# Up projection of a gated MLP by seven block products in place of eight, with the gated features kept in DRAM

## The chip, the cores and the metric

One core of a Trainium2 chip. The metric is the device time of one execution in microseconds, as the median of several runs. Engines are named as in the profile: PE is TensorE's matmul and PEld its weight load, DVE is VectorE, ACT is ScalarE, POOL is GpSimd, SP is SyncE, whose queue issues every transfer of this kernel.

## The reference

The kernel computes two layers of a diffusion backbone over 1024 latent tokens and 256 context tokens of width 1024, all in fp32. A layer is a mixing sub-layer (one input projection, four head groups, one output projection) and a channel sub-layer, both inside scaled RMS norms. Only the channel sub-layer of the latents changes:

```
def conv_ffn(h, w_up, w_conv, w_down):          # h (1024, 1024)
    u = dwconv3(h @ w_up, w_conv)               # w_up (1024, 2 * 2816), width-3 convolution over tokens
    a, b = jnp.split(u, 2, -1)
    return (jax.nn.silu(a) * b) @ w_down        # w_down (2816, 1024)
hx = rmsnorm(x, g_pre_ffn[l]) * (1 + s2_x) + sh2_x
x = x + g2_x * rmsnorm(conv_ffn(hx, ...), g_post_ffn[l])
```

The first layer does the same for the context tokens; the second layer doesn't need them.

## The kernel before

Every fp32 product is made of three TensorE passes. Both operands are split into a rounded part and a residual (`weight`, L109, for weights: ScalarE casts RAW to WH at L116, VectorE subtracts to WL at L117; `to_hk`, L247, for activations), and `project` (L286) adds hi x hi, hi x lo and lo x hi in PSUM at L291 to L293. A moving operand has 512 token columns, a stationary one 128 x 128.

**Entering the MLP.** `out_tile` (L1049) finishes the output projection of one tile of 128 tokens: norm, gate, residual sum, store to `xmid`, and the norm in front of the MLP. `to_h2` (L1085) turns four such tiles for one slice k of 128 features: four transposes on PE (L251), scale and shift on ACT (L252), cast and residual on DVE (L253, L254). The first token half is written after tiles 5 and 6 and behind the loop over tiles, the second half at its end (L1110 to L1116).

**The MLP of the latents.** The features come in 22 pairs f of 128 gate and 128 value features. `up` (L1150) computes a pair: for each of the two, `fmajor` (L295) runs two token halves of 8 slices x 3 matmuls into the two PSUM tiles G, ACT copies them out (L1158), `conv3` (L321) makes the convolution with one pass on ACT (L324) and two on DVE (L325, L326). SiLU (L1164), product (L1165) and the split of the gated features (L1167, L1168) follow; they stay in SBUF. `down` (L1233) takes groups of two pairs and, for each of the eight token tiles, adds 2 x 2 x 3 matmuls (L1174 to L1176) into a PSUM tile M2, which DVE adds to an SBUF accumulator `acc` (L1254). Up and down alternate by groups. After the last group come Square, the gate product (split between POOL and DVE, L1262) and the sum with `xmid` (L1213); the very last tile of the kernel goes by halves (`end_tile`, L1216).

**Beside it.** In the first layer `mod_pool` (L158) computes the next layer's modulation in steps between the tiles of `down`: 24 blocks of 1 MB, four matmuls each (L182). `ctx_h2` (L1135) and the loop at L1304 make the context's MLP behind that of the latents, and there the next layer's norms and transposes begin (`Prenorm`).

**Order.** The source emits instructions in the order told; the build then arranges each engine's queue from that order, the dependencies and its own estimate of when each input is ready, so that a queue's order need not be the source's. At run time a queue is worked off strictly in order. Buffers are pools of named tiles with fixed counts: RAW 3, WH and WL 4 each, G 2, HC 2.

Of the kernel before, what the change touches and what calls it, by code (L numbers as in the profile page):

```python
# [9 lines left out]
ALU = mybir.AluOpType  # L10
# [15 lines left out]
LG = 4  # L26


def build(tc, d, out, dbg=None):
# [19 lines left out]
    xmid = [[dram.t([P, D], f"xmid{l}_{t}") for t in range(NT + 2)] for l in range(DEPTH)]  # L49
    xres = [[dram.t([P, D], f"xres{l}_{t}") for t in range(NT + 2)] for l in range(DEPTH - 1)]  # L50
# [107 lines left out]
    def mod_pool(m, ts, w_tile, r_tile, ahead):  # L158

        l = m.l
        work = [(t, k) for t in ts for k in range(KT)]
        ws = {}

        def load(i):
            if i < len(work):
                t, k = work[i]
                w = ws[i] = w_tile()  # L170
                sp.dma_start(out=w, in_=d["w_mod"][l, P * k : P * k + P, 2048 * t : 2048 * t + 2048])

        for i in range(ahead):
            load(i)
        pr = None
        for i, (t, k) in enumerate(work):
            load(i + ahead)
            w = ws.pop(i)
            if k == 0:
                pr = X()  # L180
            for j in range(4):
                pe.matmul(pr[32 * j : 32 * j + 32, :], sc32[:, k, :], w[:, 512 * j : 512 * j + 512], start=(k == 0), stop=(k == KT - 1))  # L182
            yield
            if k == KT - 1:
                mr = r_tile()
                act.copy(mr, pr)
                yield
                yield
                mod_out(m, t, mr)
            else:  # L190
                yield
                yield
            yield

    def mod_out(m, t, mr):
        tp = X()
# [63 lines left out]

    def h_tiles():
        hh = [hp_.t([P, N], "H", 16, F32R) for _ in range(KT)]
        hl = [hp_.t([P, N], "H", 16, F32R) for _ in range(KT)]
        return hh, hl

    def hc_tiles():
        return hp_.t([P, KT, NC], "HC", 2, F32R), hp_.t([P, KT, NC], "HC", 2, F32R)

# [591 lines left out]
    for l in range(DEPTH):  # L860
# [136 lines left out]
        korder = [2, 3, 4, 5, 6, 7, 0, 1]  # L997
        wop = Pool(f"wo{l}", bufs=1, side="right")
        wo = {}

        def load_wo(kk, early):
# [4 lines left out]
            else:  # L1006
                hi, lo = hp_.t([P, N], "H", 16, F32R), hp_.t([P, N], "H", 16, F32R)
# [72 lines left out]
        hh2, hl2 = [], []  # L1080
        for k in range(KT):
            hh2.append(hp_.t([P, N], "H", 16, F32R))
            hl2.append(hp_.t([P, N], "H", 16, F32R))

        def to_h2(n0, k, ps):  # L1085
            ns = slice(P * n0, P * n0 + 512)
            to_hk(k, xn[n0 : n0 + 4], hh2[k][:, ns], hl2[k][:, ns], m.a2, m.mc[:, 3], 0, tmp2(), ps)
# [8 lines left out]
        for i, t in enumerate(order):  # L1096
# [13 lines left out]
            if t in (5, 6):  # L1110
                for k in (2 * t - 10, 2 * t - 9):
                    to_h2(0, k, G())
        for k in range(4, KT):
            to_h2(0, k, M2()[:, 0:512])
        for k in range(KT):
            to_h2(4, k, M2()[:, 0:512])  # L1116
# [4 lines left out]
        psum_phase(f"d{l}", X=1, M2=2, M1=1)  # L1121
        if l + 1 < DEPTH:
            m2 = mods[l + 1] = mod_cols(l + 1)
            mod_small(m2)

            it2 = mod_pool(m2, (0, 1, 2), lambda: hp_.t([P, 2048], "HC", 2), lambda: hp_.t([P, 512], "HC", 2), 1)
# [8 lines left out]
        def ctx_h2(fpool, tpool):  # L1135
# [4 lines left out]
            for i, t in enumerate((8, 9)):  # L1140
# [6 lines left out]
                     lambda: fpool.t([P, 128], "t1", 1), mx)  # L1147
# [30 lines left out]
        halves = [slice(512 * i, 512 * i + 512) for i in range(2)]  # L1178


        tpool = Pool(f"ft{l}", bufs=1, side="right")
        if with_ctx:
            cpool = Pool(f"fc{l}", bufs=1, side="right")
        fpool = Pool(f"ff{l}", bufs=1, side="left")
        tk, tkc = Tok(hh2, hl2), None
        acc = [fpool.t([P, D], "acc", NT) for t in range(NT)]
        gs, fin, ahead = {}, [], {}


        spare = not with_ctx  # L1190
        if spare:
            lp = Pool(f"lp{l}", bufs=1, side="right")

        def g_tiles(f):
            if spare and f > FF - LG:
                hc = hp_.t([P, 2, N], "HC", 2, F32R) if f < FF - 1 else lp.t([P, 2, N], "g", 1, F32R)
                return hc[:, 0], hc[:, 1]
            return fpool.t([P, N], "gh", 3, F32R), fpool.t([P, N], "gl", 3, F32R)

        def up_l(f):  # L1200
            gs[f] = up(f, tk, LAT, N, tpool, g_tiles)

        def load_x(t):
            if t < NT:
                ahead[t] = tpool.t([P, D], "T4", 3)
                sp.dma_start(out=ahead[t], in_=xmid[l][t])

        def close(t, r):

            if t not in ahead:  # L1210
                load_x(t)
            x = ahead.pop(t)
            dve.scalar_tensor_tensor(x, acc[t], r[:, 0:1], x, ALU.mult, ALU.add)  # L1213
            sp.dma_start(out=xres[l][t] if l + 1 < DEPTH else out[P * t : P * t + P], in_=x)

        def end_tile(t, pt, sq, gt2):  # L1216

            x = ahead[t]
            ss = sm.t([P, 4], "ss2")
            for i, h in enumerate(halves):  # L1220
                dve.tensor_add(acc[t][:, h], pt[:, h], acc[t][:, h])
                act.activation(sq[:, h], acc[t][:, h], AF.Square, accum_out=ss[:, i : i + 1])
            while fin:
                close(*fin.pop(0))
            for e, h in zip((pool, dve), halves):
                e.tensor_mul(acc[t][:, h], acc[t][:, h], gt2[:, h])
            dve.tensor_add(ss[:, 2:3], ss[:, 0:1], ss[:, 1:2])
            r = rstd_of(ss[:, 2:3])
            for h in halves:
                dve.scalar_tensor_tensor(x[:, h], acc[t][:, h], r[:, 0:1], x[:, h], ALU.mult, ALU.add)  # L1230
                sp.dma_start(out=out[P * t : P * t + P, h], in_=x[:, h])

        def down(fs, first, last):  # L1233
            if last:
                gt2 = fpool.t([P, D], "gh", 3)
                gate_tile(m, 1, 0, gt2)
                sq = fpool.t([P, D], "gl", 3)
                if spare:
                    load_x(0)
            wd = {f: weight(d["w_down"][l, P * f : P * f + P, :]) for f in fs}  # L1240
            for t in range(NT):
                if last and spare:
                    load_x(t + 1)
                pt = M2()
                for ns in halves:
                    for i, f in enumerate(fs):
                        down_into(pt[:, ns], ns, gs[f], wd[f], slice(P * t, P * t + P), i == 0, i == len(fs) - 1)
                if last and t == NT - 1 and l + 1 == DEPTH:
                    end_tile(t, pt, sq, gt2)
                    return  # L1250
                if first:
                    act.copy(acc[t], pt)
                else:
                    dve.tensor_add(acc[t], pt, acc[t])  # L1254
                for _ in range(2 - (t % 4 > 0)):
                    next(it2, None)
                if last:
                    ss = sm.t([P, 1], "ss")
                    act.activation(sq, acc[t], AF.Square, accum_out=ss)
                    cut = 384 if spare else 768  # L1260
                    for e, c in ((pool, slice(0, cut)), (dve, slice(cut, D))):
                        e.tensor_mul(acc[t][:, c], acc[t][:, c], gt2[:, c])  # L1262
                    fin.append((t, rstd_of(ss, tag="f")))
                    if len(fin) > DELAY:
                        close(*fin.pop(0))
            if last:
                while fin:
                    close(*fin.pop(0))

        DELAY = 2 if l + 1 < DEPTH else 1  # L1270
        n = FF - LG if spare else FF
        groups = [list(range(f, f + FG)) for f in range(0, n, FG)] + ([list(range(n, FF))] if spare else [])
        for f in groups[0]:
            up_l(f)

        for gi, fs in enumerate(groups):
            nx = groups[gi + 1] if gi + 1 < len(groups) else []
            if nx:
                up_l(nx[0])
            early = spare and gi == len(groups) - 2  # L1280
            if early:
                for f in nx[1:]:
                    up_l(f)
            if with_ctx and gi == len(groups) - 2:
                tkc = ctx_h2(fpool, tpool)
            down(fs, gi == 0, not nx)
            if not early:
                for f in nx[1:]:
                    up_l(f)
        fpool.close()  # L1290
        if spare:
            lp.close()
# [3 lines left out]
        if with_ctx:  # L1296
            nf = Prenorm(l + 1, m2, Pool(f"nm{l + 1}", bufs=1, side="left"), xres[l], mx)
# [130 lines left out]
```

## Time and profile before

| | |
|---|---|
| median of three runs | 2830.73 us (2830.61 to 2831.06) |
| the profiled execution, its own time | 2831.68 us |
| its span | 2829.8 us |
| PE busy | 2761.1 us (98%) |
| DVE, ACT, POOL busy | 1483.0, 1019.6, 130.8 us |
| share of the chain that ended last | PE 78%, DVE 4%, ACT 2%, DMA 2% |
| moved by transfers | 271.27 MB, mean 96 GB/s |

The span reaches from the first to the last instruction of the profiled execution; its own time is measured around it. A group of instructions is told as line, engine, operation, output <- input, shape, count, then busy time and mean duration of one, then the engine's idle time ahead of them. The durations of matmuls overlap, since TensorE works on several at a time. A stretch of the table of stretches is told with busy time and instructions of each engine, the granted clock of TensorE (1.00 is full), the transfer engines' share and GB/s.

### The profile page before, as it was taken

The numbers are of one execution on the slowest core, as the hardware profiler recorded it, in microseconds if no ns is written. First come the engines' busy times: TensorE is split into PE (matmuls) and PEld (weight loads), VectorE is DVE, ScalarE is ACT, GpSimd is POOL, SyncE is SP. The second block draws the span as 40 slices with busy tenths as digits, with TensorE's granted clock in tenths as the row PEclk, the third lists the DMA queues.
The fourth block names the chain that finished last, engine by engine and source line by source line (L and its number), as shares of the span: only waits on it lengthen the run. The fifth ranks groups of instructions, "written<-read, shape, count | busy, mean of one in ns | idle before, by whom it ended". The sixth has DMA issues, their size and how long they took to land.

```text
span 2829.8 us, 36199 instructions
## 1 busy us (share of the span) xinstructions
PE 2761.1 (98%) x14624; PEld 2262.9 (80%) x14624; DVE 1483.0 (52%) x2459; ACT 1019.6 (36%) x1697; POOL 130.8 (5%) x158
## 2 busy tenths in 40 slices
PE   7999999999999999999899999999999999999998
PEld 4877888887778777777789898788878888888886
DVE  5445456445344444444788754466453444544455
ACT  5222435334322222222467522345344323232331
POOL 0003000000000000000120001100000000000002
PEclk9999999999999999999999999999999999999999
DMA  6631222532222222322386520312521111111113
GB/s 250 212 117 44 64 55 53 181 131 76 90 78 83 100 88 72 95 90 59 120 271 198 178 78 20 89 45 62 195 81 52 45 53 45 52 45 52 45 51 121
DMA packets 125454, 271.27 MB, mean 96 GB/s; under 512 B 45027, under 2 KB 69094, under 8 KB 119142
## 3 DMA queue, kind: packets, MB, share of 16 engines
q1 hardware_dynamic: 125286, 268.95, 30.0%
q8 instruction: 115, 1.88, 0.3%
q14 instruction: 53, 0.43, 0.1%
HBM read 235.59 MB, written 28.34 MB: 93 GB/s over the span
## 4 chain that ended last, share of the span: by engine, by line
PE 78%; DVE 4%; ACT 2%; DMA 2%; issue 1%; POOL 1%; POOLq 0%; DVEq 0%; SPq 0%; ACTq 0%
PE G L292 15%; PE G L291 15%; PE G L293 15%; PE M L1174 6%; PE M L1175 5%; PE M L1176 5%; PE M L1047 2%; PE M L1045 2%; PE M L1046 2%; PE T L773 1%; PE G L315 1%; PE G L317 1%; PE G L316 1%; PE X L182 1%; DMA RAW<-in_w_up 1%
## 5 line engine op out<-in xcount | busy, mean ns | idle before, releaser
L291 PE MATMUL G<-H,WH 128*128 128x512 f32 x1792 | 701.2, 391 | 10.0 <-DVE nkl L677 6.0
L292 PE MATMUL G<-H,WH 128*128 128x512 f32 x1792 | 700.5, 391 | 0.2
L293 PE MATMUL G<-H,WL 128*128 128x512 f32 x1792 | 700.1, 391 | 0.0
L117 DVE TENSOR_TENSOR WL<-RAW,WH 128x1024 fp32r<-128x1024 f32 x242 | 294.3, 1223 | 583.2 <-ACT WH L116 582.5
L116 ACT CAST WH<-RAW 128x1024 fp32r<-128x1024 f32 x242 | 252.1, 1051 | 652.5 <-PE G L292 395.8
L291 PEld LDWEIGHTS G<-H,WH 128*128 128x128 f32 x1792 | 336.5, 188 | 79.3 <-issue 10.9
L292 PEld LDWEIGHTS G<-H,WH 128*128 128x128 f32 x1792 | 336.6, 188 | 69.3 <-DVE H L254 1.9
L293 PEld LDWEIGHTS G<-H,WL 128*128 128x128 f32 x1792 | 336.5, 188 | 67.7 <-issue 0.5
L1174 PE MATMUL M<-WH,gh 128*128 128x512 f32 x744 | 296.1, 398 | 7.5 <-DVE acc L1254 5.7
L1175 PE MATMUL M<-WL,gh 128*128 128x512 f32 x744 | 292.5, 393 | 0.7 <-DVE WL L117 0.7
L1176 PE MATMUL M<-WH,gl 128*128 128x512 f32 x744 | 292.3, 393 | 0.3 <-DVE gl L1168 0.3
L1254 DVE TENSOR_TENSOR acc<-M,acc 128x1024 f32<-128x1024 f32 x151 | 184.3, 1221 | 126.8 <-PE M L1176 125.5
L1174 PEld LDWEIGHTS M<-WH,gh 128*128 128x128 f32 x744 | 140.6, 189 | 56.7 <-issue 17.6
L1158 ACT COPY T<-G 128x512 f32<-128x512 f32 (+1 forms) x220 | 117.7, 535 | 147.3 <-PE G L293 146.6
L1176 PEld LDWEIGHTS M<-WH,gl 128*128 128x128 f32 x744 | 140.9, 189 | 30.9 <-DVE gl L1168 0.9
L1175 PEld LDWEIGHTS M<-WL,gh 128*128 128x128 f32 x744 | 140.5, 189 | 29.5 <-DVE WL L117 1.6
L325 DVE SCALAR_TENSOR_TENSOR T<-T,fcw,T 128x1023 f32<-128x1023 f32 (+1 forms) x132 | 134.0, 1015 | 38.3 <-ACT T L324 38.3
L293 PE MATMUL G<-HC,WL 128*128 128x256 f32 x496 | 140.5, 283 | 0.9 <-DVE WL L117 0.8
L291 PE MATMUL G<-HC,WH 128*128 128x256 f32 x496 | 140.7, 284 | 0.3 <-ACT WH L116 0.3
L292 PE MATMUL G<-HC,WH 128*128 128x256 f32 x496 | 140.9, 284 | 0.0
L326 DVE SCALAR_TENSOR_TENSOR T<-T,fcw,T 128x1023 f32<-128x1023 f32 (+1 forms) x132 | 134.1, 1016 | 4.0
L324 ACT ACTIVATE T<-T,fcw 128x1024 f32<-128x1024 f32 (+1 forms) x132 | 123.6, 936 | 12.5 <-DVE T L326 8.5
(338 smaller groups left out, 3973.8 us busy)
## 6 DMA issues: line engine op xcount, KB each, us to landing
RAW<-in_w_up SPq DMA_DIRECT2D x132, 512.0 KB, 3.7
RAW<-in_w_down SPq DMA_DIRECT2D x66, 512.0 KB, 3.6
HC<-in_w_mod SPq DMA_DIRECT2D x24, 1024.0 KB, 5.0
RAW<-in_w_in SPq DMA_DIRECT2D x44, 512.0 KB, 3.6
mw<-in_w_mod SPq DMA_DIRECT2D x16, 1024.0 KB, 5.4
T<-xmid SPq DMA_DIRECT2D x20, 512.0 KB, 4.1
xmid<-x SPq DMA_DIRECT2D x18, 512.0 KB, 2.6
x<-xres SPq DMA_DIRECT2D x18, 512.0 KB, 4.2
```

The costliest lines, as they stand in the source:

```text
L116: act.copy(hi, raw)
L117: dve.tensor_sub(lo, raw, hi.bitcast(F32))
L291: pe.matmul(o, hi[:, wk], tok.cols(k, 0, c), start=(k == 0), stop=False)
L292: pe.matmul(o, hi[:, wk], tok.cols(k, 1, c), start=False, stop=False)
L293: pe.matmul(o, lo[:, wk], tok.cols(k, 0, c), start=False, stop=(k == KT - 1))
L324: act.activation(dst[:, a:b], src[:, a:b], AF.Copy, scale=w[:, 1:2])
L325: dve.scalar_tensor_tensor(dst[:, a + 1 : b], src[:, a : b - 1], w[:, 0:1], dst[:, a + 1 : b], ALU.mult, ALU.add)
L326: dve.scalar_tensor_tensor(dst[:, a : b - 1], src[:, a + 1 : b], w[:, 2:3], dst[:, a : b - 1], ALU.mult, ALU.add)
L1174: pe.matmul(o, gh[:, tsl], hi[:, ns], start=start, stop=False)
L1175: pe.matmul(o, gh[:, tsl], lo[:, ns], start=False, stop=False)
L1176: pe.matmul(o, gl[:, tsl], hi[:, ns], start=False, stop=stop)
L1254: dve.tensor_add(acc[t], pt, acc[t])
```

## The change

For one pair let A = [a11 a12; a21 a22] be the gate and value columns (rows 1, 2) by the two halves of the 1024 inputs, and B the normed activations, halves of the inputs by halves of the tokens. The four blocks of the result are formed from seven products instead of eight (the Winograd form): sums of weight blocks per pair, sums of activation blocks once per layer, sums of the products per pair.

- After tiles 4 to 6 `first_half` makes slices of the first token half and stores the raw values to DRAM (`hraw`); once the last tile is there, a loop over j = 0..3 makes the second half, reads the first back and forms four sums (`t3`, `n1`, `t2`, `t4`, beside `b22`), each split into rounded part and residual (`Half.put`).
- Per pair four weight operands are prepared (`prep0`, `prepx`, `prepy`, `prepa`); the products `q1` to `q7` are 12 matmuls each, into PSUM tiles G (one bank), M2 (two banks) and M1 (one bank). `s1`, `s5` and the first result block are copied by ACT, the rest is summed by DVE.
- `gated` forms the rest of u, the convolutions (value taps negated, `fcn`), SiLU and the product, and stores the gated features to DRAM (`gscr`). u and w of a pair take the two HC buffers.
- All 22 pairs come first. The down projection then runs over token tiles (0, 1, 2), (3, 4, 5), (6, 7) with the sum over all 22 blocks in PSUM; the features are loaded and split for each group, and `w_down` is read for each group too, except eight blocks that stay in SBUF (`RES`). `acc` and its additions are gone.
- `mod_pool` computes only part (0,) of the next layer's modulation here; parts 1 and 2 move into the second layer's mixing stage, as in the first layer.

```diff
-    def mod_pool(m, ts, w_tile, r_tile, ahead):
+    def mod_pool(m, ts, w_tile, r_tile, ahead, ps=X):
...
+    class Half:
+        def __init__(self, tile):
+            self.t = [tile() for _ in range(2)]
+        def part(self, lo, j):
+            return self.t[j // 2][:, lo, 512 * (j % 2) : 512 * (j % 2) + 512]
+        def put(self, j, raw):
+            act.copy(self.part(0, j), raw)
+            dve.tensor_sub(self.part(1, j), raw, self.part(0, j).bitcast(F32))
...
-        if l == 0:
-            it = mod_pool(m, (1, 2), lambda: mw.t([P, 2048], "mw", 2), lambda: mw.t([P, 512], "ma", 1), 1)
-        else:
-            it = iter(())
+        it = mod_pool(m, (1, 2), lambda: mw.t([P, 2048], "mw", 2), lambda: mw.t([P, 512], "ma", 1), 1)
...
+        def prepx(f):
+            w = pair[f]
+            ra, rb = w["r0"], w["r1"]
+            x = w["x"] = fu.t([P, 1024], "XY", 2)
+            dve.tensor_add(x[:, 0:512], ra[:, 0:512], rb[:, 0:512])
+            dve.tensor_add(x[:, 512:1024], rb[:, 0:512], rb[:, 512:1024])
+            w["s31"] = split(x, *wtiles())
...
+        def blocks(o, w, i, b, start, js=range(4)):
+            hi, lo = w
+            for j in js:
+                wk = slice(512 * i + P * j, 512 * i + P * j + P)
+                first, last = start and j == 0, j == 3
+                pe.matmul(o, hi[:, wk], b.part(0, j), start=first, stop=False, skip_group_check=True)
+                pe.matmul(o, hi[:, wk], b.part(1, j), start=False, stop=False, skip_group_check=True)
+                pe.matmul(o, lo[:, wk], b.part(0, j), start=False, stop=last, skip_group_check=True)
...
+        def q6(f, js=range(4)):
...
+                dve.tensor_sub(w["v"], w["s1"], w["b"])
+                dve.tensor_add(w["z"], w["v"], w["cd"][:, 512:1024])
+        def q3(f):
+            blocks(pair[f]["cd"][:, 0:512], pair[f]["s2s"], 1, b22, False)
+        def q4(f):
+            blocks(pair[f]["cd"][:, 512:1024], pair[f]["a22"], 0, t4, False)
+        def gated(f):
+            w = pair[f]
+            u, g, v = w["u"], w["w"], w["v"]
+            dve.tensor_tensor(u.rearrange("p a (b n) -> p (a b) n", b=2)[:, 1:3], w["cd"].rearrange("p (b n) -> p b n", b=2),
+                              v.unsqueeze(1).to_broadcast([P, 2, 512]), ALU.add)
+            dve.tensor_add(u[:, 1, 512:1024], w["z"], w["s5"])
+            conv3(g[:, 0], u[:, 0], m.fcw[:, 2 * f], [(0, N)])
+            act.activation(g[:, 0], g[:, 0], AF.Silu)
+            conv3(g[:, 1], u[:, 1], fcn[:, 2 * f + 1], [(0, N)])
+            dve.tensor_mul(g[:, 1], g[:, 0], g[:, 1])
+            sp.dma_start(out=gscr[l][f], in_=g[:, 1])
...
+        for j in range(4):
...
+            to_raw(4, j, pt[:, 0:512], s12)
+            to_raw(4, j + 4, pt[:, 512:1024], s22)
+            b22.put(j, s22)
+            dve.tensor_sub(s22, s22, s12)
+            t3.put(j, s22)
+            dve.tensor_sub(s12, s11, s12)
+            n1.put(j, s12)
+            dve.tensor_add(s11, s22, s11)
+            t2.put(j, s11)
+            dve.tensor_sub(s21, s11, s21)
+            t4.put(j, s21)
+            q7(0, (j,))
+            q5(0, (j,))
+            q6(0, (j,))
+        for f in range(FF):
+            more = f + 1 < FF
+            if f:
+                q7(f)
+            if f and more:
+                prep0(f + 1)
+            if f > 1:
+                q2(f)
+            ev2(f)
+            if f:
+                q5(f)
+                q6(f)
+            if more:
+                prepx(f + 1)
+            q3(f)
+            if f and more:
+                q1(f + 1)
+            if more:
+                prepy(f + 1)
+            q4(f)
+            if more:
+                prepa(f + 1)
+            gated(f)
...
+        for ts in ((0, 1, 2), (3, 4, 5), (6, 7)):
...
+                for i, t in enumerate(ts):
+                    for ns in halves:
+                        for f in fs:
+                            down_into(pts[i][:, ns], ns, g[f], w[f], slice(P * i, P * i + P), f == 0, f == FF - 1)
+                    if f0 == FF - FG:
+                        end_tile(t, pts[i], xt[i])
+                for _ in range(4 if n0 == 0 else 2):
                     next(it2, None)
```

## Rows read from the trace of the kernel before

**Rows 1.** The page: span, busy time of the engines, chain by engine.

```profile
span 2829.8 us, 36199 instructions
PE 2761.1 (98%) x14624; PEld 2262.9 (80%) x14624; DVE 1483.0 (52%) x2459; ACT 1019.6 (36%) x1697; POOL 130.8 (5%) x158
PE 78%; DVE 4%; ACT 2%; DMA 2%; issue 1%; POOL 1%; POOLq 0%; DVEq 0%; SPq 0%; ACTq 0%
```

**Rows 2.** The table of stretches: second layer's MLP behind its entry.

```profile
2112.00:2816.00 704.00, 704.00 (x3105) 582.36 (x3104) 335.47 (x282) 219.04 (x256) 12.96 (x12) 1.00 0.17 55
```

**Rows 3.** The timeline of PE behind the last output product: start, us, what.

```profile
2089.61 1.04 PE L251 MATMUL M<-c_ident,xn 128*128 128x128 f32 x8
2090.41 0.47 PE L291 MATMUL G<-H,WH 128*128 128x512 f32 x1
...
2091.65 1.32 PE L251 MATMUL M<-c_ident,xn 128*128 128x128 f32 x8
```

**Rows 4.** The chain of waits in the first layer's MLP: modulation.

```profile
710.92 0.99 PE X L182 x8
```

**Rows 5.** The table of stretches: mixing of layer 1; start of the context's MLP.

```profile
1664.00:1728.00 64.00, 63.82 (x517) 58.85 (x516) 35.72 (x112) 13.47 (x40) 0.12 (x1) 1.00 0.11 34
...
1408.00:1472.00 64.00, 58.88 (x376) 52.31 (x375) 54.36 (x75) 37.83 (x66) 17.09 (x14) 0.97 0.79 270
```

**Rows 6.** The page's list of transfers: loads of w_down.

```profile
RAW<-in_w_down SPq DMA_DIRECT2D x66, 512.0 KB, 3.6
```

**Rows 7.** The groups of instructions, shapes kept apart: DVE and ACT.

```profile
L117 DVE TENSOR_TENSOR WL<-RAW,WH 128x1024 fp32r<-128x1024 f32 x242 | 294.3, 1223 | 583.2 <-ACT WH L116 582.5
L116 ACT CAST WH<-RAW 128x1024 fp32r<-128x1024 f32 x242 | 252.1, 1051 | 652.5 <-PE G L292 395.8 <-PE M L1176 211.1 <-PE G L317 24.5
L1254 DVE TENSOR_TENSOR acc<-M,acc 128x1024 f32<-128x1024 f32 x151 | 184.3, 1221 | 126.8 <-PE M L1176 125.5
L325 DVE SCALAR_TENSOR_TENSOR T<-T,fcw,T 128x1023 f32<-128x1023 f32 x88 | 113.0, 1284 | 38.3 <-ACT T L324 38.3
L1158 ACT COPY T<-G 128x512 f32<-128x512 f32 x176 | 101.6, 578 | 146.1 <-PE G L293 145.9
L324 ACT ACTIVATE T<-T,fcw 128x1024 f32<-128x1024 f32 x88 | 101.4, 1152 | 3.0
L1164 ACT ACTIVATE T<-T 128x1024 f32<-128x1024 f32 x44 | 46.6, 1060 | 114.7 <-DVE T L326 114.7
L254 DVE TENSOR_TENSOR H<-t,H 128x512 fp32r<-128x512 f32 x32 | 22.1, 690 | 0.9
L252 ACT ACTIVATE t<-M,mc,a 128x512 f32<-128x512 f32 x24 | 18.1, 777 | 7.1 <-DVE H L254 7.1
```

**Rows 8.** The timeline of DVE at the entry of the second layer's MLP.

```profile
2097.05 0.75 DVE L245 TENSOR_SCALAR HC<-x,rstdp 128x1024 f32<-128x1024 f32 x1 [0.73 <-POOL rstdp L237]
...
2102.72 0.69 DVE L254 TENSOR_TENSOR H<-t,H 128x512 fp32r<-128x512 f32 x1
2103.32 0.42 DVE L253 CAST H<-t 128x512 fp32r<-128x512 f32 x1
```

**Rows 9.** The table of stretches there, L293 alone, then L251: PE, PEld.

```profile
2089.60:2112.20 22.60, 8.49 (x21) 3.97 (x22) 1.00 0.14 56
...
2089.60:2112.20 22.60, 7.65 (x48) 5.24 (x47) 1.00 0.14 56
```

**Rows 10.** The timeline of the kernel's end.

```profile
2816.08 0.40 PE L1176 MATMUL M<-WH,g 128*128 128x512 f32 x1
...
2826.11 0.99 SPq L1231 DMA_DIRECT2D out_x<-T  x2
```

**Rows 11.** The timeline of a pair in the second layer: DVE and ACT.

```profile
2143.93 1.28 DVE L325 SCALAR_TENSOR_TENSOR T<-T,fcw,T 128x1023 f32<-128x1023 f32 x1 [0.44 <-ACT T L324]
...
2147.83 1.05 ACT L1167 CAST gh<-T 128x1024 fp32r<-128x1024 f32 x1 [0.35 <-DVE T L1165]
```

More of the change, by code (lines that the diff above doesn't have):

```diff
@@ L25 @@
 FG = 2
-LG = 4
+RES = 8
 def build(tc, d, out, dbg=None):
@@ L179, in mod_pool @@
             if k == 0:
[L180 removed]
+                pr = ps()
             for j in range(4):
@@ new lines, in first_half, with S, split, wtiles @@
+        def first_half(k):
+            h = op.t([P, 512], "t5", 2)
+            to_raw(0, k, G(), h)
+            (b11 if k < 4 else b21).put(k % 4, h)
+            sp.dma_start(out=hraw[KT * l + k], in_=h)
+        pair = {f: {} for f in range(FF)}
+        def S():
+            return fu.t([P, 512], "S", 6)
+        def split(raw, hi, lo):
+            act.copy(hi, raw)
+            dve.tensor_sub(lo, raw, hi.bitcast(F32))
+            return hi, lo
+        def wtiles():
+            return wp.t([P, 1024], "WH", 4, F32R), wp.t([P, 1024], "WL", 4, F32R)
@@ new lines, in q1, with q2, ev2, q7 @@
+        def q1(f):
+            w = pair[f]
+            w["a"] = G()
+            blocks(w["a"], w["a1"], 0, b11, True)
+            w["s1"] = s1p.t([P, 512], "s1", 2)
+            act.copy(w["s1"], w["a"])
+        def q2(f):
+            blocks(pair[f]["a"], pair[f]["a1"], 1, b21, False)
+        def ev2(f):
+            w = pair[f]
+            w["u"], w["w"] = hp_.t([P, 2, N], "HC", 2), hp_.t([P, 2, N], "HC", 2)
+            act.copy(w["u"][:, 0, 0:512], w["a"])
+        def q7(f, js=range(4)):
+            w = pair[f]
+            if js[0] == 0:
+                w["cd"] = M2()
+            blocks(w["cd"][:, 512:1024], w["s31"], 0, t3, True, js)
@@ L1178, in build @@
         halves = [slice(512 * i, 512 * i + 512) for i in range(2)]
[L1181 to L1214, printed above, removed]
@@ L1219, in end_tile @@
             ss = sm.t([P, 4], "ss2")
             for i, h in enumerate(halves):
[L1221 to L1226, printed above, removed]
+                act.activation(y[:, h], pt[:, h], AF.Square, accum_out=ss[:, i : i + 1])
@@ L1229, in end_tile @@
             for h in halves:
-                dve.scalar_tensor_tensor(x[:, h], acc[t][:, h], r[:, 0:1], x[:, h], ALU.mult, ALU.add)
+                dve.scalar_tensor_tensor(x[:, h], y[:, h], r[:, 0:1], x[:, h], ALU.mult, ALU.add)
                 sp.dma_start(out=out[P * t : P * t + P, h], in_=x[:, h])
[L1233 to L1255, printed above, removed]
-                    next(it2, None)
[L1257 to L1289, printed above, removed]
```

158 lines of the change are left out of this document (128 added, 30 removed).

## The prediction

> **What bounds the kernel now.** I read the page first: TensorE is busy 98% of the span, VectorE 52%, and the chain of waits lies on TensorE for 78% [rows 1]. A busy TensorE may still wait inside, because its matmul ends are modelled, so the table of stretches comes next. In the second layer's MLP 3105 matmuls of 512 columns start in 704.0 us at granted clock 1.00, the level of 2.4 GHz [rows 2]: one per 704.0 / 3105 = 0.2267 us. The 391 ns of the groups overlap and are not used for sums. The same row has VectorE busy 335 us and ScalarE 219 us of 704, transfers at a share of 0.17: inside the MLP nothing but the number of matmuls counts. The timeline shows one thing about order: up-projection matmuls (L291) stand between transposes (L251) that the source puts wholly ahead of them [rows 3]. The build thus reorders each engine's queue around late inputs, and I count no stall for a step merely because the source writes it early.
>
> **Matmuls removed.** A feature block (a pair: gate and value column of 128) takes 2 x 2 x 8 x 3 = 96 matmuls before, and 7 products x 4 slices x 3 = 84 after: 96 x 0.2267 = 21.76 us against 19.04. Over 22 pairs and two layers 528 matmuls go: 528 x 0.2267 = **-119.7 us**. The down projection keeps its 1056 per layer, the modulation for the next layer its 96 matmuls: 64 of them move to layer 1's mixing stage (8 take 0.99 us [rows 4]: 8 us move, none goes). With them 16 loads of 1 MB move past that stage's loads on SP's queue; a stretch there has a transfer share of 0.11 [rows 5], so they hide: 0, bounds 0 to 5.
>
> **The up loop, per pair.** VectorE now forms the block sums and the output sums [rows 7]: three 1024-wide residuals 3 x 1.223, one 512-wide 0.690, four 512-wide sums of weights 2.76, v and z out of PSUM 2 x 0.69 (a PSUM operand costs nothing extra: 1.221 beside 1.223), the doubled sum into u 1.221, its last quarter 0.69, four convolution passes 4 x 1.284, the product 1.22. That is 16.8 us in 17 instructions, 88% of 19.04. ScalarE: three casts 3.15, four 512-wide copies 2.31, two convolution starts 2.30, SiLU 1.06 = 8.8 us. Neither exceeds TensorE's 19.04. What of it TensorE waits for: s5 must be copied before the third product (q3), z be taken before q4. Behind q5 and q6 stand one and two more products of 12 x 0.2267 = 2.72 us, so each has 2.7 to 5.4 us for 0.6 to 1.3 us of work. Weight sums have five products, 13.6 us. The product's store and the next weight loads share SP's queue, but RAW's three buffers come free a pair ahead, and a load lands in 3.6 us [rows 6]. One wait is new: u and w share the two HC buffers, so ScalarE's copy ev2 waits until the pair before has passed its value convolution, 8 to 9 us after that pair's q4; behind it in ScalarE's queue stands the copy of s5, which q3 needs 10.9 us after (q7, q2, q5, q6), so some 1.3 us are to spare. So the loop costs 0 beyond its matmuls; the cover is VectorE's 2.2 us of slack per pair. Bound: 0 to 1 us per pair, 44 in all.
> The 512-wide residual lasts 0.69 us, yet the next instruction starts 0.60 us after its own start [rows 8]; by starts the pair needs about 15.3 us (16.8 - 17 x 0.09).
> The Trainium skill (VectorE: DVE Perf Modes, "The DRAIN you can't avoid" and "Rules for kernel authors") says that each operation is followed by a flush of the pipe and that operations should be few; this change raises their number. By that rule the durations add up in full, 16.8, and the slack is 2.2 us; by the row's starts it would be 3.7. The trace agrees only in part: starts lie closer than durations here. The sum above uses the larger figure either way.
>
> **The start of the up phase.** Before, in the 22.6 us after the last output product, 65 matmuls (21 or 22 on each of three lines) and 48 transposes start [rows 9]: 65 x 0.2267 + 48 x 0.1 (8 from 2089.61 to 2090.41 [rows 3]) = 19.5, so 3.1 us are lost. After, the second token half needs, per slice j, five residuals and four sums of 512 on VectorE: 9 x 0.69 = 6.2 us, four times 24.8; ScalarE 2 x 0.777 + 5 x 0.578 = 4.4 [rows 7]. The first half's raw columns are stored (8 x 256 KB) beside the products of tiles 4 to 6 and read back ahead of use, on the same queue: hidden. The second half can start when the last normalised tile is there, 8.2 us after the last product (2097.05 + 0.75 against 2089.6 [rows 8]). Until then q1 and q2 of two pairs cover, 48 x 0.2267 = 10.9 us. From there TensorE has per j eight transposes and nine matmuls, 2.9 us, beside 6.2: 4 x 3.3 = 13.2 exposed. Then pair 0 still owes 8.3 us on VectorE (u, its last quarter, convolutions, product) while pair 1's weights wait behind: some 3.5 us until the slack has caught up. 16.7 - 3.1 = 13.6, taken as **+14 per layer, +28**. Bounds: -3 (the reorder hides all) to +30 per layer (24.8 plus 5.9 us of pair 0's sums exposed, nothing beside).
>
> **From up to down, and between token groups.** Down's first tiles lie where the up pool was; a cast and a residual of 384 columns (three quarters of the 512-wide 0.578 and 0.690, so 0.43 and 0.52) come after q4 of pair 21: **+2 per layer**, bounds 0 to 10 (pair 21's whole 8.3 us ahead of it). A token group's sums are read by Square, then by one fused product, some 3.5 us; the next group reaches the same PSUM buffer 2.7 to 5.4 us after its last matmul: +0.5 at each of four borders, **+2**, bound 8. The 28 further splits of w_down per layer and the gated features' splits cost per block 1.22 + 0.52 = 1.7 us of VectorE beside 4.1 (three tiles) or 2.7 us (two) of TensorE: hidden.
>
> **Transfers.** w_down is read 50 times instead of 22 per layer, the features written once (22 x 512 KB) and read back. A step of two blocks moves 2 x 512 + 2 x 192 KB in 36 x 0.2267 = 8.2 us: 177 GB/s. In layer 0 a 1 MB modulation block joins it: about 306. The last, two-tile group needs 655 KB per 2.72 us, 241. The trace has moved 270 GB/s at a share of 0.79 [rows 5], which scales to 342: it fits, narrowly. RAW has three buffers, landing 3.6 us [rows 6] plus 2.3 us of split, so one block per 2 us. I take **+3** for layer 0, bounds 0 to 12.
>
> **The end.** From the last matmul's start to the end of the span 13.7 us pass (2816.08 to 2829.8 [rows 1, 10]): sums into acc, Square, GpSimd's product, then the stores 3.7 us. After, acc and GpSimd are gone; tile 6's product and add (2.5 us), two products 1.3, the power 0.9, one fused half 0.7 and the stores give about 9.5: **-4**. The context's MLP keeps its work, 0, bounds -5 to +10.
>
> **Sum.** -119.7 + 28 + 4 + 2 + 3 - 4 = -86.7. The profiled execution took 2831.68 us, so 2745.0; the median of the runs lies 0.95 lower, hence 2744.
>
> **Rivals.**
> A. Hand-offs: a convolution waits 0.44 us for ScalarE, a cast waits 0.35 for VectorE [rows 11]. If 12 of 17 VectorE operations each wait 0.44, a pair takes 16.8 + 5.3 = 22.1 us and VectorE sets the pace: (22.1 - 19.04) x 44 = +135, 2879, slower than before. It decides from 19.04 + 86.7 / 44 = 21.0 us per pair. For it: 88% use. Against: those waits arise where VectorE has nothing else (48% idle); neighbouring pairs' sums can fill them. 0.07.
> B. The reorder hides the start, as it nearly does now: 2744 - 28 = 2716. Against it: 24.8 us of VectorE beside 11.6 of TensorE. 0.10.
> C. Late transfers: each of 66 steps loses 0.5 us: +33, 2777. For it: in the stretch of 270 GB/s the mean granted clock fell to 0.97 [rows 5], so TensorE did wait. Against: 177 GB/s in most steps. 0.08.
> D. Partial A: 1 us per pair, 2788. 0.10.
>
> **Numbers.** Forecast 2744 at 0.65. From B's 2716 less 4 to D's 2788 plus some 12 of the bounds: 2712 to 2800. 0.2% is 5.7 us, about what a measurement of this kernel can tell from no change. Faster 0.92, same 0.01, slower 0.07 (A).
>
> **What would show it.** Right: 512-column matmuls still 0.227 us apart, a pair about 19.0 us, VectorE near 85% in the up phase, clock 1.00; a dip of TensorE of some 17 us at the start of each up phase. Wrong: pairs over 20 us with TensorE waiting for v, z or s5 (A, D), waits for RAW or the features' loads in the down passes (C), no dip (B), or a mean granted clock below 1.00 outside the dip; in it I would not wonder at 0.97, as in the stretch where TensorE waited before [rows 5].

## The result and the profile after

The changed kernel takes 2803.88 us (median of four runs, 2803.63 to 2808.51) where the kernel before takes 2830.67 (2830.56 to 2831.06): 0.9909 times, 95% interval 0.9892 to 0.9926. That is faster by 27 us, not by the 87 that were forecast, and 4 us above the upper end of the range. The question is where 60 us went.

The page of the changed kernel, against [rows 1]:

```profile
span 2802.1 us, 36743 instructions
...
PE 2689.5 (96%) x14096; PEld 2175.1 (78%) x14096; DVE 1703.0 (61%) x2917; ACT 1145.5 (41%) x1925; POOL 100.6 (4%) x142
...
PE 76%; DVE 5%; ACT 2%; DMA 2%; issue 1%; POOL 0%; DVEq 0%; POOLq 0%; SPq 0%; ACTq 0%
```

TensorE starts exactly 528 matmuls fewer (14624 to 14096), so the change does what it says, yet its busy time falls by only 72 us: the matmuls that stay have become dearer. Its share falls from 98% to 96%, so it also waits more. The chain of waits now holds 5% of VectorE.

The table of stretches of the second layer's MLP (start, up loop, up to down, down; the columns are the stretch, its length, busy us and starts of PE, PEld, DVE, ACT and POOL, granted clock, DMA share, GB/s), against [rows 2]:

```profile
2080.00:2112.00 32.00, 21.65 (x81) 14.52 (x79) 24.97 (x40) 17.09 (x25) 0.55 (x1) 0.79 0.39 131
2112.00:2144.00 32.00, 29.20 (x118) 22.34 (x119) 26.00 (x34) 18.49 (x25) 0.00 (x0) 0.95 0.11 34
...
2304.00:2432.00 128.00, 128.00 (x556) 104.20 (x555) 102.72 (x115) 56.23 (x67) 0.00 (x0) 1.00 0.22 79
2528.00:2560.00 32.00, 19.02 (x73) 14.94 (x72) 21.91 (x23) 15.13 (x19) 0.00 (x0) 0.79 0.72 247
2592.00:2720.00 128.00, 127.37 (x546) 102.37 (x545) 48.92 (x61) 38.23 (x58) 1.84 (x3) 1.00 0.46 155
```

The same 128 us of MLP before the change:

```profile
2176.00:2304.00 128.00, 128.00 (x567) 105.98 (x566) 56.92 (x47) 42.10 (x48) 0.00 (x0) 1.00 0.16 50
```

Three losses can be read here. The start holds 81 and 118 matmuls in 32 us where 141 fit. Up to down holds 73. And in the steady stretches, with the clock at 1.00 and TensorE never or hardly idle, only 556 and 546 matmuls start in 128 us where 567 did. In the up loop VectorE is busy 80%, and TensorE does not wait for it.

What TensorE waits for (first rows of its waits: us in total, times, longest):

```profile
PE M L1369 <- ACT gh L1410: 25.9, 2, 13.0
PE M L1159 <- ACT H L284: 20.8, 8, 5.3
...
PE M L1159 <- DVE S L1199: 4.6, 2, 2.3
```

The first is one wait per layer, of the first down product for its cast features. The second belongs to the four slices at the start of each up phase. The third is q4 of pair 21 waiting for z. The timeline of the start, second layer (start, us, engine, line, tiles, idle time before it and what ended it):

```profile
2106.63 1.46 DVE L285 TENSOR_TENSOR HX<-S,HX 128x512 fp32r<-128x512 f32 x2
...
2107.26 1.05 PE L1159 MATMUL M<-HX,WH 128*128 128x512 f32 x2
...
2108.11 0.84 PE L1102 MATMUL M<-c_ident,HC 128*128 128x128 f32 x3
...
2110.12 0.78 ACT L1103 ACTIVATE S<-M,mc,a 128x512 f32<-128x512 f32 x1 [2.76 <-PE M L1102]
2110.93 0.62 ACT L284 CAST H<-S 128x512 fp32r<-128x512 f32 x1
...
2111.58 0.69 DVE L285 TENSOR_TENSOR H<-S,H 128x512 fp32r<-128x512 f32 x1 [3.50 <-ACT H L284]
```

VectorE, which was to set the pace here, stands still for 3.50 us: it waits for ScalarE's cast, which waits for the transposes (L1102) of the next slice, and these stand among and behind the products of this slice on TensorE. The timeline from up to down, first layer:

```profile
1102.92 1.28 DVE L344 SCALAR_TENSOR_TENSOR HC<-HC,fcn 128x1023 f32<-128x1023 f32 x1
...
1104.28 0.33 SPq L232 DMA_DIRECT2D gt<-grow  x1
1104.70 0.86 SPq L1408 DMA_DIRECT2D gr<-gscr  x2
...
1109.13 0.96 ACT L1410 CAST gh<-gr 128x384 fp32r<-128x384 f32 x2 [4.38 <-DMA gr<-gscr]
...
1109.70 0.80 PE L1369 MATMUL M<-WH,gh 128*128 128x512 f32 x1 [12.90 <-ACT gh L1410]
...
1110.71 0.63 PE L1371 MATMUL M<-WH,gl 128*128 128x512 f32 x1
1111.14 0.63 PE L1369 MATMUL M<-WH,gh 128*128 128x512 f32 x1
1111.57 0.63 PE L1370 MATMUL M<-WL,gh 128*128 128x512 f32 x1
...
1114.56 0.39 PE L1369 MATMUL M<-WH,gh 128*128 128x512 f32 x1
1114.80 0.40 PE L1370 MATMUL M<-WL,gh 128*128 128x512 f32 x1
```

The gate row's tile gt lies where fcn lay, so its load leaves SP's queue only when the last tap that reads fcn is through (1102.92 + 1.28), and the loads of the gated features stand behind it in that queue. Behind the wait of 12.90 us the products start 0.43 us apart, the level of 1.2 GHz, until 1113.7.

The end, against [rows 10]:

```profile
2792.35 0.40 PE L1371 MATMUL M<-WH,gl 128*128 128x512 f32 x1
...
2798.37 0.99 SPq L1396 DMA_DIRECT2D out_x<-x  x2
```

From the last matmul's start to the end of the span it is 2802.1 - 2792.35 = 9.75 us, where it was 13.7.

### The profile page after: what moved, and what is told of

The parts are those of the page before. It is cut to its first block, busy times and chain, and to the rows that moved or that the text cites. A ratio compares the mean times of both kernels' runs of the same rounds, so it can differ in the third digit from the quotient of the medians.

```text
span 2802.1 us, 36743 instructions
## 1 busy us (share of the span) xinstructions
PE 2689.5 (96%) x14096; PEld 2175.1 (78%) x14096; DVE 1703.0 (61%) x2917; ACT 1145.5 (41%) x1925; POOL 100.6 (4%) x142
## 4 chain that ended last, share of the span: by engine, by line
PE 76%; DVE 5%; ACT 2%; DMA 2%; issue 1%; POOL 0%; DVEq 0%; POOLq 0%; SPq 0%; ACTq 0%
PE M L1160 7%; PE M L1161 7%; PE M L1159 7%; PE M L1369 6%; PE M L1371 6%; PE M L1370 6%; PE G L309 4%; PE G L310 4%; PE G L311 4%; PE G L1160 3%; PE G L1159 3%; PE G L1161 3%; PE M L1063 2%; PE M L1064 2%; PE M L1062 2%; PE T L791 1%
## 5 line engine op out<-in xcount | busy, mean ns | idle before, releaser
L1369 PE MATMUL M<-WH,gh 128*128 128x512 f32 x536 | 216.1, 403 | 28.8 <-ACT gh L1410 25.9
L1411 DVE TENSOR_TENSOR gl<-gr,gh 128x384 fp32r<-128x384 f32 (+1 forms) x132 | 66.9, 511 | 260.5 <-ACT gh L1410 258.3
L1371 PE MATMUL M<-WH,gl 128*128 128x512 f32 x536 | 213.4, 398 | 1.0 <-DVE gl L1363 1.0
L1370 PE MATMUL M<-WL,gh 128*128 128x512 f32 x536 | 213.4, 398 | 0.0
L1159 PE MATMUL M<-H,WH 128*128 128x512 f32 x352 | 140.1, 399 | 26.1 <-ACT H L284 20.8
L309 PE MATMUL G<-H,WH 128*128 128x512 f32 x384 | 153.7, 400 | 10.1 <-DVE nkl L695 6.0
L310 PE MATMUL G<-H,WH 128*128 128x512 f32 x384 | 152.4, 397 | 0.0
L311 PE MATMUL G<-H,WL 128*128 128x512 f32 x384 | 152.3, 397 | 0.0
L1160 PE MATMUL M<-HX,WH 128*128 128x512 f32 x352 | 143.3, 407 | 0.4 <-DVE HX L285 0.2
L1160 PE MATMUL M<-H,WH 128*128 128x512 f32 x352 | 140.8, 400 | 1.3 <-DVE H L285 1.3
L1161 PE MATMUL M<-HX,WL 128*128 128x512 f32 x352 | 142.0, 403 | 0.0
L1159 PE MATMUL M<-HX,WH 128*128 128x512 f32 x352 | 141.4, 405 | 0.0
L1161 PE MATMUL M<-H,WL 128*128 128x512 f32 x352 | 139.7, 397 | 0.0
L1160 PE MATMUL G<-H,WH 128*128 128x512 f32 x352 | 137.8, 392 | 0.0
```

Of the source, the lines that this page charges most:

```text
L309: pe.matmul(o, hi[:, wk], tok.cols(k, 0, c), start=(k == 0), stop=False)
L310: pe.matmul(o, hi[:, wk], tok.cols(k, 1, c), start=False, stop=False)
L311: pe.matmul(o, lo[:, wk], tok.cols(k, 0, c), start=False, stop=(k == KT - 1))
L1159: pe.matmul(o, hi[:, wk], b.part(0, j), start=first, stop=False, skip_group_check=True)
L1160: pe.matmul(o, hi[:, wk], b.part(1, j), start=False, stop=False, skip_group_check=True)
L1161: pe.matmul(o, lo[:, wk], b.part(0, j), start=False, stop=last, skip_group_check=True)
```

## The experiments

The chips of the experiments ran the kernel before in 2832.6 to 2834.2 us, so times are compared by ratio, and kernels that ran once by stretches of their traces. All of these come from the matmuls' starts, in us, first / second layer: "start" from the last out product to the 85th product of the up phase, the time in which 84 products begin, as many as q1 and q2 of two pairs and the 36 sliced ones (the build draws some products of pair 1 ahead of the last sliced ones); "pause" from the last up to the first down product; "spacing" the mean distance of neighbouring 512-column matmuls of both layers (distances of 0.20 to 0.26 us only); "MLP" from the last out to the last down product.

| kernel | start | pause | spacing up / down | MLP |
|---|---|---|---|---|
| changed | 45.4 / 44.5 | 13.3 / 13.4 | 0.2306 / 0.2334 | 734.1 / 717.2 |
| e1_align | 44.1 / 44.4 | 13.5 / 13.2 | 0.2271 / 0.2270 | 724.2 / 707.2 |
| e2_gate_late | 45.3 / 44.6 | 9.0 / 8.9 | 0.2306 / 0.2333 | 732.7 / 716.1 |
| e3_first_group | 45.5 / 45.2 | 1.7 / 2.0 | 0.2306 / 0.2332 | 724.6 / 705.6 |
| e4_start | 35.3 / 36.2 | 13.5 / 13.7 | 0.2305 / 0.2333 | 723.6 / 710.5 |
| e5_offsets | 45.0 / 44.3 | 14.4 / 13.3 | 0.2273 / 0.2319 | 730.0 / 712.5 |
| e7_all_three | 35.1 / 35.7 | 0.2 / 0.2 | 0.2273 / 0.2271 | 705.5 / 689.6 |
| e8_all_store_late | 34.9 / 35.0 | 0.2 / 0.2 | 0.2273 / 0.2270 | 700.4 / 686.5 |
| e9_by_256 | 44.4 / 45.4 | 13.3 / 13.5 | 0.2272 / 0.2270 | 724.5 / 710.0 |
| e10_by_128 | 44.3 / 46.4 | 13.2 / 13.2 | 0.2293 / 0.2326 | 729.5 / 717.4 |
| e11_by_32 | 44.1 / 44.3 | 14.3 / 13.4 | 0.2300 / 0.2333 | 732.0 / 715.6 |

**The spacing.** By the built programs' memory maps, weights (WH, WL) and H tiles start at byte 416 modulo 512 in both kernels, and so did gh, gl and half of the yh tiles before. The change drops six small tiles of 32 bytes, so all that is opened behind them starts 192 bytes earlier (gh and gl at 224), and fcn, 528 bytes long, shifts HX and W3 once more (to 256). First the paddings alone:

```diff
     dve.memset(halfneg, -0.5)
+    for i in range(2):
+        for _ in range(3):
+            dve.memset(sm.t([P, 4], f"pad{i}"), 0.0)
...
-        fcn = fu.t([P, 2 * FF, 3], "fcn", 1)
+        fcn = fu.t([P, 256], "fcn", 1)[:, : 6 * FF].rearrange("p (a b) -> p a b", b=3)
```

> The changed kernel with two paddings and nothing else: 192 bytes more in the small-tile pool, so that the tiles opened behind it start again at the byte (modulo 512) at which they start in the kernel before and at which the weights and H tiles start; and the negated taps fcn take 1024 bytes in place of 528, so that HX, W3H and W3L start at that byte too. Theory (the matmuls' spacing depends on where their operands lie): the down products' mean spacing falls from 0.2333 to about 0.227, the up products' with HX from 0.232 to 0.236 to about 0.228; 1056 down products x 0.0063 = 6.7 us, 792 up products x 0.0065 = 5.1 us and 1 to 2 us of the out projection, so 12 to 14 us for each layer and a time of about 2777 us. The 13.3 us between the last up and the first down matmul stay. Rival (the spacing comes from the transfers and evictions of the new loops, wherever the tiles lie): spacings and time as in the changed kernel, 2804 us.

Measured: 2781.1 us, ratio 0.9819 (0.9803 to 0.9835) where the changed kernel has 0.9909: 0.0090 x 2831 = 25 us, 20.0 of them in the two MLP stretches of the table. The stretches of up loop and down phase, second layer of e1:

```profile
2290.00:2418.00 128.00, 128.00 (x561) 104.32 (x560) 102.72 (x115) 54.71 (x66) 0.00 (x0) 1.00 0.24 80
2574.00:2702.00 128.00, 127.06 (x561) 104.95 (x560) 50.41 (x63) 40.73 (x62) 1.82 (x3) 1.00 0.48 159
```

In the down phase 561 matmuls start in place of 546, while VectorE's work and the transfers stay nearly as they were. So it is the place of the operands, not the traffic. Products with HX and WL, at 0.2364 the dearest, are at 0.2267 as well. The same shift, put into the kernel before:

```diff
     dve.memset(halfneg, -0.5)
+    for _ in range(2):
+        dve.memset(sm.t([P, 4], "pad", 2), 0.0)
```

> The kernel before with 64 bytes more in the small-tile pool (two tiles that are set to zero once and read by nothing), so that every tile opened behind it moves by 64 bytes against the weights, as the 192 bytes fewer did in the changed kernel modulo 256; nothing else. Theory: the down products' spacing rises from 0.228 to 0.233, 2112 x 0.0055 = 11.6 us, with 1 to 2 us of the out projection 12 to 14 us more, 1.0042 to 1.005 times the kernel before. Rival (the spacing belongs to the changed kernel's loops): within 0.1% of the kernel before.

Measured: 2845.55 us against 2833.53, ratio 1.0042 (1.0025 to 1.0059), the mean spacing of its down products 0.2333 in place of 0.2280. Two tiles that nothing reads cost 12 us. Which distances are harmful was tried first within one kernel:

```diff
-                    gh, gl = g[f] = dn.t([P, n], "gh", 6, F32R), dn.t([P, n], "gl", 6, F32R)
+                    gh, gl = g[f] = [dn.t([P, 392], x, 6, F32R)[:, :n] for x in ("gh", "gl")]
```

> The kernel of e1_align with the tiles gh and gl made 1568 bytes long in place of 1536, so that the twelve of them start 0, 32, 64 and so on to 352 bytes (modulo 512) behind the place at which the weights start; nothing else. Theory (the spacing of down products follows the distance of the two operands modulo a power of two): tiles at distance 0 keep 0.2267 us, those at other distances 0.231 to 0.236, and the table by distance shows the modulus: if it is 256, the tile at distance 256 has 0.227 again. Rival (e1's gain came from elsewhere, as from the length of the rows or another order of the work): all twelve tiles 0.227.

A miss: all twelve tiles lay between 0.230 and 0.236, gh at distance 0 too (0.2319), and gl at distance 256 had 0.2323. So a product's spacing does not depend on its own two operands alone; the table by distance could not be read off, and the modulus stayed open. So all tiles were moved together, by 256, 128 and 32 bytes, with 8, 4 or 1 more small tiles:

```diff
+    for _ in range(8):
+        dve.memset(sm.t([P, 4], "more", 8), 0.0)
```

> The kernel of e1_align with 256 bytes more in the small-tile pool, so that all tiles behind it (gh, gl, HX, W3H, W3L, yh among them) start 256 bytes off the place of the weights and H tiles, modulo 512; nothing else. e5 left the modulus open, as its twelve tiles lay at different places next to one another. Theory with modulus 256: down spacing 0.227, span as e1_align's, 2778. Theory with modulus 512: 0.230 to 0.236, span about 2790 to 2800.

> As e9, but 128 bytes off. Theory with modulus 128: down spacing 0.227 and span 2778. With modulus 256 or 512: 0.230 to 0.236, span about 2790 to 2800.

> As e9, but 32 bytes off, the smallest step that the pools take. Any modulus above 32: down spacing 0.230 to 0.236, span about 2790 to 2800. If the spacing were 0.227, small distances would be harmless and only large ones cost.

The down phase, 128 us of the second layer, in e9:

```profile
2580.00:2708.00 128.00, 127.06 (x561) 104.87 (x561) 51.86 (x65) 41.16 (x63) 1.83 (x3) 1.00 0.49 160
```

in e10:

```profile
2592.00:2720.00 128.00, 127.39 (x547) 102.75 (x547) 49.34 (x62) 39.16 (x60) 1.82 (x3) 1.00 0.48 158
```

and in e11:

```profile
2590.00:2718.00 128.00, 127.37 (x546) 102.31 (x546) 49.67 (x63) 39.40 (x60) 1.83 (x3) 1.00 0.48 158
```

561, 547 and 546: of the distances tried, 256 bytes cost nothing, while 128 and 32 cost as much as the 192 of the changed kernel. The spans are 2782.4, 2799.0 and 2796.4 us. That of e9 is 4.6 us above e1's 2777.8 with the same spacing, but its time of 2784.22 us lies within e1's four (2779.30 to 2785.66).

The memory maps and the traces show two things more. In the out projection of the kernel before, products with wo, which starts at byte 480, come twelve in a row. With yh at 416 the last two of the twelve are still 0.231 and 0.232 us apart; with yh at 480 they have come to 0.2268 and 0.2264, from 0.2343 at the third (means by place in the row). So byte 480 is not bad in itself, the distance counts, and after a change of distance up to ten products pass until the spacing has settled. In the same way q4 of the changed kernel, whose operands W3 and HX both start at byte 256, goes from 0.2358 (the first of its twelve) to 0.2266 (the eleventh). In e5 the distance changes after every one or two products, which fits that no tile there came to 0.227.

**From up to down.** First the gate row's load alone, moved behind:

```diff
         gt2 = dn.t([P, D], "gt", 1)
-        gate_tile(m, 1, 0, gt2)
...
                 if f0 == FF - 3 * FG:
+                    if n0 == 0:
+                        gate_tile(m, 1, 0, gt2)
```

> The changed kernel with the load of the gate row gt2 issued late, before the x loads of the first token group's third-last step, into the same tile; nothing else. Theory A (the gate load, first in SP's queue and waiting for fcn's last reader, is alone what holds the first gr loads): the first down matmul starts 3 to 5 us after the last up matmul in place of 13.3, in both layers, 2786 us. Theory B (behind that stands pair 21's own tail: gl is split on VectorE behind the taps and the product of pair 21, which end about 10 us after the last up matmul): the pause falls only to 8 to 11 us, 2795 to 2800 us. Rival (gr's own place over XY and W3H holds its loads): 13 us as before, 2804 us.

Measured: pauses of 9.0 and 8.9 us, theory B; 2802.59 us. TensorE's waits there and ScalarE's work ahead of the first, first layer (timeline):

```profile
1102.25 1.05 ACT L1215 ACTIVATE HC<-HC 128x1024 f32<-128x1024 f32 x1
1103.21 0.91 ACT L1409 CAST gh<-gr 128x384 fp32r<-128x384 f32 x2
...
1103.75 0.79 PE L1369 MATMUL M<-WH,gh 128*128 128x512 f32 x1 [8.59 <-DVE H L1419]
...
1106.49 0.80 PE L1371 MATMUL M<-WH,gl 128*128 128x512 f32 x1 [1.52 <-DVE gl L1410]
```

The split of w_down (H) named in the first wait is no operand of that product; gh is, and its cast stands behind pair 21's SiLU (L1215) in ScalarE's queue. In the second layer the wait, 8.46 us, is put down to that cast. The MLP is shorter by only 1.4 and 1.1 us, as a second wait follows, ended 11.7 us after the last up product, for gl behind pair 21's tail. So the gate load was the last of the obstacles, not the only one. Then the first two blocks in tiles that pair 21 does not hold:

```diff
+                    first = n0 == 0 and f0 == 0
-                    gr = dn.t([P, n], "gr", 4)
+                    gr = raw_tile()[:, :n] if first else dn.t([P, n], "gr", 4)
...
+                    gh, gl = g[f] = [x[:, :n] for x in wtiles()] if first else (...)
```

> As the kernel with the late gate load, and the first two gated blocks of the first token group go through RAW, WH and WL tiles in place of gr, gh and gl, so that their loads and splits wait for nothing that pair 21 still uses. Theory (the pause is head-of-line blocking in SP's, ACT's and VectorE's queues, not missing data): the first down matmul follows the last up matmul by under 2.5 us; the 36 products of the first two blocks (8.2 us) cover the tail of pair 21, and at most 3 us come back as a second pause before blocks 2 and 3; 8 to 12 us less for each layer, 2780 to 2788 us. Rival (the tail of pair 21, 8 to 9 us of VectorE, has to be paid somewhere): the pause moves behind the first 36 products with nearly its whole length, 2798 to 2804 us.

Measured: pauses of 1.7 and 2.0 us, the MLP 9.5 and 11.7 us shorter, 2781.67 us. TensorE's waits, first layer:

```profile
1094.15 0.50 PE L1369 MATMUL M<-WH 128*128 128x512 f32 x1 [1.32 <-DVE HC L1211]
...
1105.24 1.62 PE L184 MATMUL G<-HC,sc 128*32 128x512 f32 x8 [2.63 <-DMA HC<-in_w_mod]
...
1107.84 0.79 PE L1369 MATMUL M<-H,gh 128*128 128x512 f32 x1 [0.98 <-ACT gh L1410]
```

The 36 products cover pair 21's tail; of the pause some 3.6 us come back in layer 0 and 1.3 in layer 1.

**The start.** The transposes of the next slice go ahead of the products of this one, and two of the four S tiles of a slice come first:

```diff
+        raws(0)
         for j in range(4):
-            pt = M2()
-            s11, s21, s12, s22 = (S() for _ in range(4))
...
             t4.put(j, s21)
+            if j < 3:
+                raws(j + 1)
             q7(0, (j,))
```

> The changed kernel with the start of the up phase in another order: the transposes and evictions of the next slice are issued ahead of the nine products of this one, and each slice takes its tiles in the order s12, s22, s11, s21, so that two of them are free early; nothing else. Theory (each slice waits 3.1 to 3.5 us on VectorE because the next slice's transposes stand behind the products on TensorE): the stretch from the last out product to the end of the 36 sliced products, 45.4 and 44.5 us, falls by 8 to 12 us in each layer, 2781 to 2788 us. Rival (VectorE's 24.8 us of sums and splits set the stretch in any order): less than 3 us per layer, 2798 to 2804 us.

Measured: 35.3 and 36.2 us for the start, 2786.54 us. The stretch from 672 to 704 us of the first layer, in which the start of the changed kernel ends (at 684.6) and that of e4 has just ended (at 674.6), in e4:

```profile
672.00:704.00 32.00, 31.31 (x135) 24.87 (x134) 29.93 (x40) 15.63 (x21) 0.00 (x0) 1.00 0.20 66
```

and in the changed kernel:

```profile
672.00:704.00 32.00, 28.72 (x111) 21.27 (x110) 22.04 (x31) 16.06 (x24) 0.00 (x0) 0.87 0.12 39
```

TensorE starts 135 matmuls there in place of 111, and the clock stays at 1.00. Within e4's start VectorE, once it has the last normalised tile (647.1), waits a single time, for a load (timeline):

```profile
652.74 0.69 DVE L1136 TENSOR_TENSOR XY<-RAW 128x512 f32<-128x512 f32 x1 [1.29 <-DMA RAW<-in_w_up]
```

What is left of the start is VectorE's own work, to which weight sums of pairs 0 and 1 (XY) belong: the products of the fourth slice end only 42.1 and 43.0 us after the last out product (52.0 and 51.1 in the changed kernel), and the build puts products of pair 1 ahead of them.

**All together.** e7 holds the edits of e1, e3 and e4, and e8 these as well:

```diff
-                for _ in range(4 if n0 == 0 else 2):
+                for _ in range((4 if f0 > FG else 0) if n0 == 0 else 2):
                     next(it2, None)
...
+                if n0 == 0 and f0 == FG:
+                    sp.dma_start(out=gscr[l][FF - 1], in_=glast[:, 1])
```

> The paddings of e1_align, the late gate load and first group of e3_first_group, and the order of e4_start together. Theory (three separate losses that add up): less than the changed kernel by 25 + 22 + 17 = 64 us, 2740 us on a chip where the kernel before takes 2831 (ratio 0.968), near the forecast of 2744. Rival (they share the same waiting, as where a quicker start only leaves VectorE further behind): 2755 to 2770 us.

> As e7_all_three, with two steps moved at the start of the down projection: the steps of the next layer's modulation begin with the third pair of blocks, not the first, and pair 21's store of its gated block is issued behind the gr loads of blocks 2 and 3. Theory (the second pause that e3_first_group shows, 3.0 us before a modulation product and 2.0 us before the next down product in layer 0, 1.4 us in layer 1, is the gr loads standing in SP's queue behind the modulation's load and that store): 4 to 6 us less than e7_all_three, 0.002 of its time. Rival (gl waits for pair 21's tail on VectorE): within 1 us of e7_all_three.

Measured: e7 2742.87 us, ratio 0.9681 (0.9666 to 0.9695); e8 2738.65 us, ratio 0.9666 (0.9651 to 0.9680). The three losses add up: by the MLP stretches e1, e3 and e4 save 20.0, 21.2 and 17.3 us alone, 58.5 in sum, and e7 saves 56.3. By times e8 is 4.2 us below e7, by the MLP stretches 8.1; the two ratios' intervals overlap, so the times alone don't settle it. The waits show where it went: in layer 0, behind the first 36 products, TensorE waited 4.90 us for the modulation's load in e7,

```profile
1091.77 1.94 PE L187 MATMUL G<-HC,sc 128*32 128x512 f32 x8 [4.90 <-DMA HC<-in_w_mod]
```

and 1.16 and 1.03 us for gh and gl in e8:

```profile
1087.85 0.50 PE L1382 MATMUL M<-H,gh 128*128 128x512 f32 x1 [1.16 <-ACT gh L1423]
...
1090.31 0.50 PE L1384 MATMUL M<-H,gl 128*128 128x512 f32 x1 [1.03 <-DVE gl L1424]
```

In the second layer, which has no modulation, the wait for gh stays (2.41 us in e7, 2.50 in e8), and only that for gl, 1.04 us in e7, is gone. The two moves of e8 were not tried one by one.

## Why the prediction was wrong, step by step

- **Matmuls removed, -119.7.** The number was right, and 0.2267 us is what a matmul of the kernel before took. The step that failed is the sentence that inside the MLP nothing but the number of matmuls counts: it took the price of the remaining ones as fixed. With the tiles moved it is 0.2306 and 0.2334; e1 gets 25 us back, and e6 shows that the place alone costs the kernel before 12. No row of before was read for it, though [rows 2] gives the price for one placement only; the out projection, whose products already lay at two placements, would have shown both prices: products of H, at byte 416, were 0.227 us apart with yh at 416 and 0.233 with yh at 480.
- **Up loop, 0.** Right. In the 128 us shown 556 matmuls are 6.6 pairs, and VectorE is busy 102.72 / 6.6 = 15.5 us for each. That is near the figure by starts (15.3), not by durations (16.8). The prediction took the Trainium skill (VectorE: DVE Perf Modes, "The DRAIN you can't avoid") to say that durations add up in full; that section also says that a next operation which is not held starts earlier, and the trace agrees with that. A pair takes 128 / 6.6 = 19.4 us without a wait, so rivals A and D fall. The one wait of the phase behind its start, 2.3 us of q4 of pair 21 for z, comes from splits of w_down that the build places ahead of it; the forecast named no work of the next phase in this queue.
- **Start, +14 per layer.** Mechanism right, size off. The forecast's 10.9 us of cover and 4 x 6.2 us of VectorE make 35.7 us for the 84 products of the start; measured were 45.4 and 44.5. The step that failed is to charge VectorE's work without a wait, with transposes and products side by side: each slice's transposes stood behind the products of the one before. With that undone (e4) it is 35.3 and 36.2. That this meets the 35.7 is in part luck: VectorE also makes weight sums there, which the value put at nothing, so that the slices end 6 to 7 us later than reckoned, and products of pair 1, which the sum did not have there, fill the gap. Against it, of the 3.5 us for pair 0's tail next to nothing shows: e4 starts 135 matmuls in its 32 us there, where 139 fit at 0.2305. Net some 6 us per layer too little; rival B falls.
- **From up to down, +2 per layer, bounds 0 to 10.** Wrong, beyond the bound. The upper bound was pair 21's tail ahead of the first cast and split, and that alone is 9.0 and 8.9 us (e2). Missed was the gate row's load, which waits for a tile at fcn's place and heads SP's queue, 4.4 us more. The value +2 took the split's own work and not what stands ahead of it in three queues. Behind it the clock fell to the level of 1.2 GHz for some nine products.
- **Borders, transfers.** The largest pause in the second layer's down phase is 1.0 us. In the first layer's, e8 moves 337 GB/s while TensorE stays busy all 32 us, as this row of its stretches shows, so rival C falls too:

```profile
1092.00:1124.00 32.00, 32.00 (x148) 24.62 (x147) 12.17 (x15) 10.32 (x15) 0.00 (x0) 1.00 0.94 337
```

- **The end, -4.** Right: 13.7 to 9.75 us. The moved modulation was not separated by any run.

In sum: spacing 25, start 2 x 6 and from up to down 2 x 11 make 59 of the 60 us by which the forecast missed. With the three undone the kernel takes 0.9681 x 2831 = 2741 us, beside the forecast of 2744. That they lie so near is in part luck: e7's pause of 0.2 us in place of 2 and the tail of pair 0 make some 9 us less than was forecast, and against them stand waits behind the first 36 products that it did not name, 4.90 us for the modulation's load in the first layer, 2.41 and 1.04 for gh and gl in the second.

## What to carry to other kernels

A change that opens, drops or resizes a small tile moves everything behind it; look at where both operands of the matmuls start before and after, and pad until all operands of a run of products start at the same byte modulo 256, which cost nothing here. A single pair of tiles at a good distance among others gained little (e5, q4 of the changed kernel). At the border of two phases list what each in-order queue holds ahead of the first instruction that the next phase needs, the DMA queue above all: one load into a reused place holds all behind it. Where two engines pass slices to and fro, issue the next slice's first step ahead of this slice's last.

## What was not expected of the hardware

- The spacing of 512-column fp32r matmuls depends on where their operands lie: 0.2267 us where the starts of all operands in a run of products differ by multiples of 256 bytes, mostly 0.230 to 0.236 at distances of 32, 64, 128 and 192, with no wait and a granted clock of 1.00. After a change of distance it took up to ten products to settle (wo with yh, q4), and in a mixed sequence (e5) no tile had a mean of 0.227. What in the chip does it was not tried.
- The Trainium skill (TensorE: Matmul & The Clock Gate, "Wait — 56ns, not 53.3ns?") gives 426.7 ns at the lower and 215.7 ns at the upper level for 512 columns. The trace agrees with the first (0.43 behind the pause); at the upper level no placement tried here settled below 0.2265 us, so the measured value was the one to use.
- A wait of 1.32 us (e3) left the products behind it 0.23 us apart at once; one of 12.90 us was followed by nine at 0.43. The length of the wait alone does not decide it: behind q4's wait of 2.29 us for z in the changed kernel seven products, from the fourth on, started 0.43 us apart in the first layer and none in the second.
